# Last products of a two-layer encoder: token tile 0 through one unit sooner, its norm between tile 1's adds, part of tile 1's norm on TensorE, and another order of the first loads

## The chip, the core and the metric

The kernel runs on one core of a Trainium2 chip. The metric is device microseconds (us) of one execution, median of several runs; lower is better. All times are in us unless ns is written.

The engines: PE is TensorE's matrix product, PEld its weight load, DVE is VectorE, ACT is ScalarE, POOL is GpSimd, SP is SyncE, which issues most of the transfers (DMAs).

## The reference, cut to what matters

Two post-norm residual layers over 16 learned tokens and 256 frames of width 2048. Layer 0 mixes gated linear attention and stick-breaking attention, layer 1 is a state-space mixer. Each layer projects the tokens in, mixes, projects out, adds the result to the scaled input and normalizes:

```python
for layer in range(DEPTH):
    f = _even_mixer(h, ...) if layer % 2 == 0 else _odd_mixer(h, ...)
    h = _layer_norm(DEEPNORM_ALPHA * h + f, ln_g[layer], ln_b[layer])
return h[:, PREFIX:]

def _layer_norm(x, g, b):
    mu = jnp.mean(x, -1, keepdims=True)
    xc = x - mu
    var = jnp.mean(xc * xc, -1, keepdims=True)
    return xc * lax.rsqrt(var + LN_EPS) * g + b

def _odd_mixer(...):          # its end: 8 groups of 512 values each
    y = _rms_norm_groups(y * jax.nn.silu(z), norm_w, SSM_GROUPS)
    return jnp.einsum('bte,ed->btd', y, w_out)
```

The change touches two places: the very first projections of layer 0, and the last output products of layer 1 with the last layer norm.

## The kernel before

All matrix products are made from two parts of each float32 operand: a high part, which ACT copies into the format fp32r (`split_into`, line 146), and the low rest, which DVE or POOL subtracts (line 147). Three products, high-high, high-low and low-high, stand for one. The weights are cut into units of 128 x 2048 float32 (1 MB); a unit is loaded into one of three `raw` buffers, split in two halves of 1024 columns, and used by PE. The split of unit i+1 is emitted beside the products of unit i (`units`, line 390 on), and unit i+2 is loaded.

A planner that simulates the program orders the instructions of each engine; the order in the code is only a priority, unless it is pinned.

**The start** (`layer0`, line 258). ACT's queue issues the first 256 columns of units 0 to 2. SP's queue issues x rows 0 and 1 (one row is 128 of the 2048 input values for all tokens), then columns 256 to 512 of the three units, then rows 2 and 3 ("x1" in line 274), rows 4 and 5 ("x2"), the second quarter of each unit, and so on. The loop over c splits what has come and makes the products of two rows with three units. Before it, constants are set up: small tiles that POOL fills and, at line 311, 16 copies on DVE.

**The end** (`tail`, line 1209). Layer 1's output projection has 8 groups of 4 units; a unit gives 512 columns of the output, for two tiles of 128 tokens. `out1_half` (line 466) makes the products of half a unit for one tile, `out1_add` (line 480) adds the PSUM result, scaled per token, to the accumulator `acc`. For all groups but the last a unit serves both tiles before the next unit comes. In the last four units (i0 to i0+3, group g = 7) tile 0 goes through all four first, then tile 1. Each add is followed by `bn_stats`; after the fourth add the mean and variance are gathered (`bn_aggr`), the reciprocal deviation r comes from Ln and Exp on ACT and one Newton step of three DVE operations (line 253 on), and the 2048 columns are normalized in up to three pieces: columns c1 by two `scalar_tensor_tensor` on DVE (center: subtract the mean, times lg; scale: times r, plus lb), columns c0 by ACT (times r, minus mean times r) and then POOL (times lg, plus lb), columns c2 by ACT and then DVE. For tile 0, c0 and c1 have 1024 columns each; for tile 1, c0 has 320, c1 832 and c2 896. Each piece is stored by a DMA from SP's queue. Tile 1's last unit is made in two halves of 256 columns (`b`).

Products rotate through four PSUM buffers (`pj`); two more (`po`) serve smaller products.

## Time and profile before

| what | us |
| --- | --- |
| median of 3 runs (lowest to highest) | 1405.85 (1404.2 to 1406.54) |
| the profiled execution | 1404.02 |
| its span in the trace | 1402.3 |
| PE busy in the span | 1382.8 (99%) |
| DVE busy | 1024.5 (73%) |
| ACT busy | 769.0 (55%) |
| POOL busy | 324.2 (23%) |

Times within the trace count from the span's start. A row of a group gives an engine, an operation, its output and inputs, a count, the busy time and the mean of one; behind the bar stands how long the engine was idle before it and for whom it waited. PE's products are pipelined, so the end of one overlaps the start of the next.

### The profile page before, as it was taken

How to read it: one execution, taken by the hardware profiler on the slowest of the kernel's cores; microseconds unless marked ns; L12 is line 12 of the kernel's file. 1: busy time of each engine (PE TensorE's matmuls, PEld its weight loads, DVE VectorE, ACT ScalarE, POOL GpSimd, SP SyncE). 2: the span in 40 equal slices, each digit the busy share in tenths (PEclk: the TensorE clock that was granted, in tenths of full speed). 3: DMA queues.
4: the chain of work that ended last, by engine and by line, in shares of the span. 5: the costliest groups of instructions: out<-in, count | busy, mean ns of one | idle time of the engine just before them, and what ended most of it. 6: DMA issues, size and time to landing. Idle time of an engine off the chain costs nothing.

```text
span 1402.3 us, 26080 instructions
## 1 busy us (share of the span) xinstructions
PE 1382.8 (99%) x10701; PEld 1329.7 (95%) x10701; DVE 1024.5 (73%) x1663; ACT 769.0 (55%) x1138; POOL 324.2 (23%) x285
## 2 busy tenths in 40 slices
PE   9999999999999999999999999999999999999996
PEld 8999999999999999999999899899898999989985
DVE  7857575575565675558799989777887768778687
ACT  6645454364345544545587766555555565565651
POOL 0000110100101100114402325342332433424323
PEclk9999999999999999999999999999999999999998
DMA  9544444445444445444444755655556456454651
GB/s 326 183 153 165 168 155 176 165 167 172 159 172 160 151 154 192 156 155 142 151 151 172 265 175 192 213 192 178 207 175 227 154 192 218 161 204 149 222 196 61
DMA packets 37720, 249.84 MB, mean 178 GB/s; under 512 B 4256, under 2 KB 6112, under 8 KB 9184
## 3 DMA queue, kind: packets, MB, share of 16 engines
q1 hardware_dynamic: 37168, 247.77, 50.7%
q8 instruction: 84, 1.38, 0.4%
q10 hardware_dynamic: 432, 0.39, 0.1%
q14 instruction: 36, 0.29, 0.1%
HBM read 245.94 MB, written 2.20 MB: 177 GB/s over the span
## 4 chain that ended last, share of the span: by engine, by line
PE 83%; DVE 7%; ACT 4%; issue 2%; POOL 2%; DMA 1%; ACTq 0%; SPq 0%; POOLq 0%; DVEq 0%
PE pj L166 21%; PE pj L165 21%; PE pj L167 21%; PE pj L476 4%; PE pj L477 4%; PE pj L478 4%; DVE wlo L147 2%; PE po L1172 2%; ACT whi L146 1%; PE po L590 1%; DVE xlo L816 1%; POOL wlo L147 1%; DMA ebc<-edr 1%; DMA hacc<-in_xT 1%; POOL xt L1010 1%
## 5 line engine op out<-in xcount | busy, mean ns | idle before, releaser
L165 PE MATMUL pj<-xhi,whi 128*128 128x272 f32 (+4 forms) x2560 | 734.2, 287 | 1.5 <-ACT xhi L317 0.5
L166 PE MATMUL pj<-xlo,whi 128*128 128x272 f32 (+4 forms) x2560 | 731.3, 286 | 0.0
L167 PE MATMUL pj<-xhi,wlo 128*128 128x272 f32 (+4 forms) x2560 | 729.8, 285 | 0.0
L147 DVE TENSOR_TENSOR wlo<-raw,whi 128x1024 fp32r<-128x1024 f32 (+2 forms) x405 | 514.2, 1273 | 244.8 <-ACT whi L146 243.2
L146 ACT ACTIVATE whi<-raw 128x1024 fp32r<-128x1024 f32 (+2 forms) x435 | 451.1, 1038 | 396.4 <-PE pj L166 329.7
L165 PEld LDWEIGHTS pj<-xhi,whi 128*128 128x128 f32 x2560 | 481.6, 188 | 4.9 <-ACT whi L146 1.7
L166 PEld LDWEIGHTS pj<-xlo,whi 128*128 128x128 f32 x2560 | 482.6, 189 | 1.5 <-issue 0.6
L167 PEld LDWEIGHTS pj<-xhi,wlo 128*128 128x128 f32 x2560 | 482.0, 188 | 0.5 <-issue 0.4
L165 PE MATMUL pj<-mixh,whi 128*128 128x272 f32 x384 | 111.2, 291 | 1.0 <-ACT mixh L801 1.0
L167 PE MATMUL pj<-mixh,wlo 128*128 128x272 f32 x384 | 110.7, 289 | 0.0
L166 PE MATMUL pj<-mixl,whi 128*128 128x272 f32 x384 | 110.7, 289 | 0.0
L147 POOL TENSOR_TENSOR wlo<-raw,whi 128x1024 fp32r<-128x1024 f32 x30 | 75.7, 2524 | 118.7 <-ACT whi L146 118.5
L476 PE MATMUL pj<-whi,yh 128*128 128x512 f32 (+1 forms) x244 | 94.8, 388 | 0.0
L478 PE MATMUL pj<-whi,yl 128*128 128x512 f32 (+1 forms) x244 | 94.2, 386 | 0.0
L477 PE MATMUL pj<-wlo,yh 128*128 128x512 f32 (+1 forms) x244 | 94.2, 386 | 0.0
L248 POOL TENSOR_TENSOR gr<-gr,gsc 128x1088 f32<-128x1088 f32 x6 | 15.4, 2570 | 302.6 <-ACT gsc L247 302.6
L165 PEld LDWEIGHTS pj<-mixh,whi 128*128 128x128 f32 x384 | 72.2, 189 | 1.3 <-ACT mixh L801 1.1
L166 PEld LDWEIGHTS pj<-mixl,whi 128*128 128x128 f32 x384 | 72.3, 188 | 0.2
L167 PEld LDWEIGHTS pj<-mixh,wlo 128*128 128x128 f32 x384 | 72.3, 188 | 0.1
L485 DVE SCALAR_TENSOR_TENSOR acc<-pj,rr,acc 128x512 f32<-128x512 f32 (+1 forms) x65 | 46.1, 734 | 15.2 <-PE pj L478 15.1
L478 PEld LDWEIGHTS pj<-whi,yl 128*128 128x128 f32 x244 | 45.8, 188 | 9.2
L476 PEld LDWEIGHTS pj<-whi,yh 128*128 128x128 f32 x244 | 45.8, 188 | 9.1
(327 smaller groups left out, 1518.7 us busy)
## 6 DMA issues: line engine op xcount, KB each, us to landing
raw<-in_wts SPq DMA_DIRECT2D x212, 1024.0 KB, 4.8
ebc<-edr SPq DMA_DIRECT2D x8, 1664.0 KB, 6.4
raw<-in_wts SPq DMA_DIRECT2D x9, 256.0 KB, 5.7
hacc<-in_xT SPq DMA_DIRECT2D x7, 272.0 KB, 5.4
early<-in_wts SPq DMA_DIRECT2D x2, 512.0 KB, 7.1
lg<-in_lnr SPq DMA_DIRECT2D x1, 1024.0 KB, 4.5
lb<-in_lnr SPq DMA_DIRECT2D x1, 1024.0 KB, 4.5
out_h<-acc SPq DMA_DIRECT2D x2, 512.0 KB, 2.6
```

The costliest lines, as they stand in the source:

```text
L146: self.nc.scalar.activation(hi, src, AF.Copy)
L147: eng.tensor_tensor(lo, src, hi.bitcast(F32), op=ALU.subtract)
L165: mm(ps, whi, xhi, start=first, stop=False)
L166: mm(ps, whi, xlo, start=False, stop=False)
L167: mm(ps, wlo, xhi, start=False, stop=last)
L248: mul(c, c, e, op=ALU.mult)
L476: mm(ps, yh[:, kk, tt], hi[:, k, :], start=kk == 0, stop=False)
L477: mm(ps, yh[:, kk, tt], lo[:, k, :], start=False, stop=False)
L478: mm(ps, yl[:, kk, tt], hi[:, k, :], start=False, stop=kk == 3)
L485: self.nc.vector.scalar_tensor_tensor(a, ps, r[:, t : t + 1], a, op0=ALU.mult, op1=ALU.add)
L590: mm = lambda r, a, b, start=False, stop=False: self.nc.tensor.matmul(o[:, r], a, b, start=start, stop=stop, skip_group_check=True)
L1172: mm(o[i * 64 : (i + 1) * 64, jj, t0:S], xd[:, s, h * 64 : (h + 1) * 64], M[:, h, c0:c1], start=(s, jj) == (0, 0), stop=False, **gk,)
```

## The change

**Last products.** The unit before the last four (i0-1, the last of group 6) joins the tail: tile 0 goes through five units in a row, then tile 1. Five units are split ahead; the second half of unit i0 is put into two tiles of the old `xts` buffers and is subtracted on DVE, not POOL.

**Tile 0's norm** is a generator (`first_tile`) that is stepped after each of tile 1's adds: behind the last add of tile 0 the statistics, centering of columns 768 to 1408, Newton's step, ACT on columns 0 to 768 and POOL's two operations on them; behind the add of unit i0-1, centering of 1408 to 2048 and scaling of 768 to 1408; behind that of i0, tile 1's columns 0 to 512 times lg (`times_lg`) and the scaling of tile 0's 1408 to 2048; behind that of i0+1, tile 1's columns 512 to 768 times lg.

**Tile 1's norm.** Columns 0 to 768, already multiplied by lg, are finished on PE: the identity times acc, plus diag(-mean) times lg, plus diag(sd) times lb, in PSUM; ACT multiplies by r when it copies them out, and issues their DMAs from its own queue. DVE centers and scales the other 1280 columns.

**Order.** `keep_order` chains all DVE and all ACT instructions from tile 0's last unit on in the order of the code.

**First loads.** Rows 2 and 3 of x are issued before columns 256 to 512 of the weights, in one DMA as before; the constants are set up behind the split of the third round (`issue_after`).

The diff, with the body of the moved setup cut:

```diff
--- before.py
+++ after.py
@@ -121,6 +121,19 @@
         while self.side:
             self.tick()
 
+    def traced(self):
+        return self.tc.nc.cur_bb.bb.instructions
+
+    def keep_order(self, first):
+
+        ins = self.traced()
+        n0 = next(n for n in reversed(range(len(ins))) if ins[n] is first)
+        free = mybir.DependencyInfo(mybir.DependencyClass.NoSync, mybir.DependencyReason.DATA)
+        for eng in (mybir.EngineType.DVE, mybir.EngineType.Activation):
+            mine = [i for i in ins[n0:] if i.engine == eng]
+            for a, b in zip(mine, mine[1:]):
+                self.tc.add_manual_dep(b, a.name, free, reason="keep_order")
+
 
     def load_unit(self, i, q=None):
         if i >= NU:
@@ -269,9 +282,10 @@
             nc.scalar.dma_start(self.raw[u][:, :256], self.wts[u][:, :256])
         for kt in range(2):
             nc.sync.dma_start(self.hacc[:, kt, :], self.xT[:, kt, :])
+        nc.sync.dma_start(self.hacc[:, 2:4, :], self.xT[:, 2:4, :])
         for u in range(NS):
             nc.sync.dma_start(self.raw[u][:, 256:512], self.wts[u][:, 256:512])
-        for kind, n in ("x1", "x2", "w1", "x3", "x4", "w2", "x5", "x6", "w3", "x7"):
+        for kind, n in ("x2", "w1", "x3", "x4", "w2", "x5", "x6", "w3", "x7"):
             if kind == "x":
                 r = slice(2 * int(n), 2 * int(n) + 2)
                 nc.sync.dma_start(self.hacc[:, r, :], self.xT[:, r, :])
@@ -285,30 +299,6 @@
         self.load_wg2(0)
         nc.sync.dma_start(self.cpk[:, :C_END], self.cpk_d)
         nc.sync.dma_start(self.dta, self.dta_d)
-
-        self.nones_r, self.nL_r = [lp.tile([P, P], F32R, tag=n, name=n) for n in ("nones", "nL")]
...
-        for q in range(4):
-            for r in range(4):
-                vec.tensor_copy(add4[32 * q : 32 * q + 32, 32 * r : 32 * r + 32], self.ident[32 * q : 32 * q + 32, 32 * q : 32 * q + 32])
         self.guT = lp.tile([P, T], F32, tag="gsq", name="guT")
         self.guS = lp.tile([96, T], F32R, tag="guS", name="guS")
         ps = [self.pj() for _ in range(NS + 1)]
@@ -337,9 +327,36 @@
                 if c % 2 == 0:
                     for u in range(NS):
                         w_parts(u, c * 256, c * 256 + 512)
+            if c == 2:
+                mark = next(i for i in reversed(self.traced()) if i.engine == mybir.EngineType.DVE)
             for u in range(NS):
                 for kt in (2 * c, 2 * c + 1):
                     self.first_kt(ps[u][:, :T], u, kt)
+        with self.tc.issue_after(mark):
+
+            self.nones_r, self.nL_r = [lp.tile([P, P], F32R, tag=n, name=n) for n in ("nones", "nL")]
...
+            for q in range(4):
+                for r in range(4):
+                    vec.tensor_copy(add4[32 * q : 32 * q + 32, 32 * r : 32 * r + 32], self.ident[32 * q : 32 * q + 32, 32 * q : 32 * q + 32])
 
         for kt in range(KT):
             o = ps[NS][32 * (kt % 4) : 32 * (kt % 4) + 32, :T]
@@ -881,7 +898,7 @@
         nc.vector.memset(self.xd2, 0.0)
         self.rstd1 = {}
         self.first1()
-        self.units(len(L0), L1[:-4], {n: None for n in range(NFIRST)})
+        self.units(len(L0), L1[:-5], {n: None for n in range(NFIRST)})
         self.tail()
 
     def first1(self):
@@ -1210,16 +1227,21 @@
 
         nc, lp = self.nc, self.lp
         vec, pool = nc.vector, nc.gpsimd
+        act, mm = nc.scalar.activation, nc.tensor.matmul
         i0, g = NU - 4, NG - 1
         self.drain()
+        self.load_unit(i0 + 1)
+        self.split_half(i0, 0)
+        hi, lo = [lp.tile([P, 1024], F32R, tag="xts", name=self.nm("late"), bufs=2) for _ in range(2)]
+        self.split_into(self.raw[i0][:, 1024:], hi, lo, vec)
+        self.parts[i0, 1] = (hi, lo)
         self.load_unit(i0 + 2)
         for n, dq in enumerate((1, 2)):
             for h in range(2):
                 src = self.raw[i0 + dq][:, h * 1024 : (h + 1) * 1024]
                 o = slice((2 * n + h) * 1024, (2 * n + h + 1) * 1024)
                 hi, lo = [a.rearrange("p k t -> p (k t)")[:, o] for a in self.xrows]
-                nc.scalar.activation(hi, src, AF.Copy)
-                vec.tensor_tensor(lo, src, hi.bitcast(F32), op=ALU.subtract)
+                self.split_into(src, hi, lo, vec)
                 self.parts[i0 + dq, h] = (hi, lo)
             if n == 0:
                 self.load_unit(i0 + 3)
@@ -1229,43 +1251,107 @@
         nc.sync.dma_start(lb, self.lnr_d[1].partition_broadcast(P))
         for h in range(2):
             self.split_half(i0 + 3, h)
+
+        nid, dm = [lp.tile([P, P], F32, tag="ys2", name=self.nm("diag"), bufs=2) for _ in range(2)]
+        dsd = lp.tile([P, P], F32, tag="yu", name="dsd", bufs=2)
+        act(nid, self.ident, AF.Copy, scale=-1.0)
+        out = [self.out[t * P : (t + 1) * P, :] for t in range(2)]
+        accs = [self.acc[:, t, :] for t in range(2)]
+        sts = [lp.tile([P, 8, 6], F32, tag="fst", name=self.nm("fst"), bufs=2) for _ in range(2)]
+        mvs = [lp.tile([P, 2], F32, tag="fmv", name=self.nm("fmv"), bufs=2) for _ in range(2)]
+        sc = [[lp.tile([P, 1], F32, tag=f"f{n}", name=self.nm("f"), bufs=2) for n in range(4)] for _ in range(2)]
+
+        def center(t, a, b):
+            c = slice(a, b)
+            vec.scalar_tensor_tensor(
+                accs[t][:, c], accs[t][:, c], mvs[t][:, 0:1], lg[:, c], op0=ALU.subtract, op1=ALU.mult
+            )
+
+        def scale(t, a, b):
+            c = slice(a, b)
+            vec.scalar_tensor_tensor(accs[t][:, c], accs[t][:, c], sc[t][1], lb[:, c], op0=ALU.mult, op1=ALU.add)
+            nc.sync.dma_start(out[t][:, c], accs[t][:, c])
+
+        def times_lg(a, b):
+            vec.tensor_tensor(accs[1][:, a:b], accs[1][:, a:b], lg[:, a:b], op=ALU.mult)
+
+        def moments(t):
+            v, r, _, _ = sc[t]
+            vec.bn_aggr(mvs[t], sts[t])
+            vec.tensor_scalar(v, mvs[t][:, 1:2], LN_EPS, None, op0=ALU.add)
+            act(r, v, AF.Ln)
+            act(r, r, AF.Exp, scale=-0.5)
+
+        def first_tile():
+
+            N0, N1 = 768, 1408
+            v, r, tm, mr = sc[0]
+            moments(0)
+            center(0, N0, N1)
+            self.newton(r, v, tm)
+            vec.scalar_tensor_tensor(mr, mvs[0][:, 0:1], -1.0, r, op0=ALU.mult, op1=ALU.mult)
+            a = accs[0][:, :N0]
+            act(a, a, AF.Identity, bias=mr, scale=r)
+            pool.tensor_tensor(a, a, lg[:, :N0], op=ALU.mult)
+            pool.tensor_tensor(a, a, lb[:, :N0], op=ALU.add)
+            nc.sync.dma_start(out[0][:, :N0], a)
+            yield
+            center(0, N1, D)
+            scale(0, N0, N1)
+            yield
+            times_lg(0, 512)
+            scale(0, N1, D)
+            yield
+            times_lg(512, NP)
+            yield
+
+
+        NP = 768
+        side = None
         for t in range(2):
-            st = lp.tile([P, 8, 6], F32, tag="fst", name=self.nm("fst"), bufs=2)
-            acc = self.acc[:, t, :]
-            for dq in range(4):
-                halves = (0, 1) if t == 1 and dq == 3 else (None,)
-                for b in halves:
+            for dq in range(-1, 4):
+                u, gg = (i0 + dq, g) if dq >= 0 else (i0 - 1, g - 1)
+                col = dq % 4
+                if (t, dq) == (0, 3):
+                    first = self.traced()[-1]
+                for b in (0, 1) if (t, dq) == (1, 3) else (None,):
                     ps = self.pj()
                     for h in range(2):
-                        self.out1_half(ps, g, t, *self.parts[i0 + dq, h], h, b)
-                    self.out1_add(ps, g, t, dq, b)
-                    with self.tc.high_priority():
+                        self.out1_half(ps, gg, t, *self.parts[u, h], h, b)
+                    self.out1_add(ps, gg, t, col, b)
+                    if dq >= 0:
                         for c in range(2) if b is None else (b,):
-                            vec.bn_stats(st[:, 2 * dq + c, :], acc[:, dq * 512 + c * 256 : dq * 512 + (c + 1) * 256])
-            mv = lp.tile([P, 2], F32, tag="fmv", name=self.nm("fmv"), bufs=2)
-            v, r, tm, mr = [lp.tile([P, 1], F32, tag=f"f{n}", name=self.nm("f"), bufs=2) for n in range(4)]
-            with self.tc.high_priority():
-                vec.bn_aggr(mv, st)
-                vec.tensor_scalar(v, mv[:, 1:2], LN_EPS, None, op0=ALU.add)
-                nc.scalar.activation(r, v, AF.Ln)
-                nc.scalar.activation(r, r, AF.Exp, scale=-0.5)
-                self.newton(r, v, tm)
-                vec.scalar_tensor_tensor(mr, mv[:, 0:1], -1.0, r, op0=ALU.mult, op1=ALU.mult)
-            cut = (0, 1024, 2048, 2048) if t == 0 else (0, 320, 1152, 2048)
-            c0, c1, c2 = [slice(a, b) for a, b in zip(cut, cut[1:])]
-            vec.scalar_tensor_tensor(acc[:, c1], acc[:, c1], mv[:, 0:1], lg[:, c1], op0=ALU.subtract, op1=ALU.mult)
-            for c, eng in ((c0, pool), (c2, vec)):
-                if c.stop > c.start:
-                    a = acc[:, c]
-                    nc.scalar.activation(a, a, AF.Identity, bias=mr, scale=r)
-            vec.scalar_tensor_tensor(acc[:, c1], acc[:, c1], r, lb[:, c1], op0=ALU.mult, op1=ALU.add)
-            nc.sync.dma_start(self.out[t * P : (t + 1) * P, c1], acc[:, c1])
-            for c, eng in ((c0, pool), (c2, vec)):
-                if c.stop > c.start:
-                    a = acc[:, c]
-                    eng.tensor_tensor(a, a, lg[:, c], op=ALU.mult)
-                    eng.tensor_tensor(a, a, lb[:, c], op=ALU.add)
-                    nc.sync.dma_start(self.out[t * P : (t + 1) * P, c], a)
+                            vec.bn_stats(sts[t][:, 2 * dq + c, :], accs[t][:, dq * 512 + c * 256 : dq * 512 + (c + 1) * 256])
+                if t == 1 and side is not None:
+                    next(side, None)
+                if (t, dq) == (0, 3):
+                    side = first_tile()
+                    next(side)
+
+        acc, mv = accs[1], mvs[1]
+        v, r, tm, sd = sc[1]
+        qs = [slice(512, NP), slice(0, 512)]
+        pss = [self.po()[:, : q.stop - q.start] for q in qs]
+        pin = self.tc.keep_in_program_order
+        for ps, q in zip(pss, qs):
+            pin(mm(ps, self.ident, acc[:, q], start=True, stop=False))
+        moments(1)
+        act(dm, nid, AF.Copy, scale=mv[:, 0:1])
+        center(1, NP, 1216)
+        self.newton(r, v, tm)
+        vec.tensor_tensor(sd, v, r, op=ALU.mult)
+        act(dsd, self.ident, AF.Copy, scale=sd)
+        for d, a, l in ((dm, lg, False), (dsd, lb, True)):
+            for ps, q in zip(pss, qs):
+                pin(mm(ps, d, a[:, q], start=False, stop=l))
+        center(1, 1216, 1664)
+        center(1, 1664, D)
+        scale(1, NP, 1408)
+        scale(1, 1408, D)
+        for ps, q in zip(pss, qs):
+            act(acc[:, q], ps, AF.Copy, scale=r)
+            nc.scalar.dma_start(out[1][:, q], acc[:, q])
+        self.keep_order(first)
 
 
 def _pack(i):
```

## Rows read from the trace of the kernel before

**Rows 1.** The page: busy time, share of the span, instructions.
```profile
PE 1382.8 (99%) x10701; PEld 1329.7 (95%) x10701; DVE 1024.5 (73%) x1663; ACT 769.0 (55%) x1138; POOL 324.2 (23%) x285
```

**Rows 2.** Chain of waits, 1389 to 1403: start, us, engine, tile, line.
```profile
1390.92 0.49 DVE acc L485
...
1396.97 1.63 DVE acc L1267
```

**Rows 3.** DMA issues, 1330 to 1403: count, KB each, us to landing.
```profile
out_h<-acc SPq DMA_DIRECT2D x1, 448.0 KB, 2.7
```

**Rows 4.** Timeline of DVE and ACT at the end: start, us, operation [idle before].
```profile
1377.17 0.75 DVE L485 SCALAR_TENSOR_TENSOR acc<-pj,rr,acc 128x512 f32<-128x512 f32 x1 [1.19 <-PE pj L478]
...
1379.89 0.75 DVE L485 SCALAR_TENSOR_TENSOR acc<-pj,rr,acc 128x512 f32<-128x512 f32 x1 [1.18 <-PE pj L478]
1380.67 0.75 DVE L1244 BATCH_NORM_STATS2 fst<-acc 128x6 f32<-128x256 f32 x2
...
1381.94 1.27 DVE L1256 SCALAR_TENSOR_TENSOR acc<-acc,fmv,lg 128x1024 f32<-128x1024 f32 x1
...
1392.37 1.07 DVE L1256 SCALAR_TENSOR_TENSOR acc<-acc,fmv,lg 128x832 f32<-128x832 f32 x1
...
1392.72 0.20 ACT L1251 ACTIVATE f<-f 128x1 f32<-128x1 f32 x1
...
1393.74 0.16 DVE L255 SCALAR_TENSOR_TENSOR f<-f,f 128x1 f32<-128x1 f32 x1
```

**Rows 5.** Groups by shape, DVE and ACT: count, busy us, mean ns, idle before.
```profile
L253 DVE TENSOR_TENSOR f<-f 128x1 f32<-128x1 f32 x2 | 0.3, 150 | 0.0
L1266 DVE TENSOR_TENSOR acc<-acc,lg 128x896 f32<-128x896 f32 x1 | 1.1, 1092 | 0.8 <-ACT acc L1260 0.8
...
L943 ACT ACTIVATE acc<-po 128x512 f32<-128x512 f32 x8 | 4.7, 586 | 0.0
L544 ACT ACTIVATE ke<-ge 128x128 f32<-128x128 f32 x8 | 2.4, 302 | 0.0
L1260 ACT ACTIVATE acc<-acc,f,f 128x1024 f32<-128x1024 f32 x1 | 1.2, 1247 | 2.7 <-DVE f L1253 2.7
```

**Rows 6.** Chain of waits, 0 to 40: one float32 product, in two passes.
```profile
31.17 0.46 PE po L351 x2
```

**Rows 7.** Timelines of POOL and DVE: operations that overlap on both engines.
```profile
1361.98 2.83 POOL L147 TENSOR_TENSOR wlo<-raw,whi 128x1024 fp32r<-128x1024 f32 x1 [7.94 <-ACT whi L146]
1362.46 2.37 DVE L253 TENSOR_TENSOR rt<-rr 128x2 f32<-128x2 f32 x1
...
1368.44 3.53 POOL L147 TENSOR_TENSOR wlo<-raw,whi 128x1024 fp32r<-128x1024 f32 x1 [3.63 <-ACT whi L146]
...
1386.47 3.07 POOL L1266 TENSOR_TENSOR acc<-acc,lg 128x1024 f32<-128x1024 f32 x1 [14.50 <-ACT acc L1260]
1388.05 0.75 DVE L485 SCALAR_TENSOR_TENSOR acc<-pj,rr,acc 128x512 f32<-128x512 f32 x1
1389.62 2.38 POOL L1267 TENSOR_TENSOR acc<-acc,lb 128x1024 f32<-128x1024 f32 x1
```

**Rows 8.** Windows: busy us by engine, PE's granted clock, DMA share, GB/s.
```profile
1393.00:1393.50 0.50, 0.00 (x0) 0.00 (x0) 0.50 (x2) 0.00 (x0) 0.00 (x0) 0.96 1.07 442
1393.50:1394.00 0.50, 0.00 (x0) 0.00 (x0) 0.40 (x4) 0.00 (x0) 0.00 (x0) 0.50 0.99 410
```

**Rows 9.** The start: chain of waits, windows (PE, PEld, DVE, ACT, POOL), DVE's copies.
```profile
4.50 5.42 DMA hacc<-in_xT
...
11.92 0.39 PE pj L165
...
5.00:8.00 3.00, 2.47 (x15) 1.83 (x14) 2.94 (x14) 2.22 (x7) 0.00 (x0) 1.00 1.00 311
16.00:24.00 8.00, 8.00 (x64) 7.42 (x62) 5.47 (x8) 5.47 (x8) 0.00 (x0) 1.00 1.05 407
...
3.07 1.76 DVE L311 COPY add<-ident 32x32 f32<-32x32 f32 x16
```

More of the change, by code (lines that the diff above doesn't have):

```diff
@@ L342, in layer0 @@
                     self.first_kt(ps[u][:, :T], u, kt)
+        with self.tc.issue_after(mark):
+            self.nones_r, self.nL_r = [lp.tile([P, P], F32R, tag=n, name=n) for n in ("nones", "nL")]
+            nones, nL = [lp.tile([P, T], F32, tag="gs2", name=n, bufs=2)[:, :P] for n in ("nones_f", "nL_f")]
+            nc.gpsimd.memset(nones, -1.0)
+            nc.gpsimd.affine_select(
+                out=nL, in_=nones, compare_op=ALU.is_ge, fill=0.0, base=0, pattern=[[-1, P]], channel_multiplier=1
+            )
+            self.spad = lp.tile([P, 432], F32, tag="spad", name="spad")
+            v2 = [lp.tile([80, 512], F32R, tag=f"v2{i}", name=f"v2{i}") for i in range(2)]
+            s2 = [lp.tile([80, 1, 16], F32R, tag=f"s2{i}", name=f"s2{i}") for i in range(2)]
+            self.v2, self.s2 = v2, s2
+            self.sp2, self.nL2 = [lp.tile([48, n, 16], F32R, tag=t, name=t) for n, t in ((2, "sp2"), (1, "nL2"))]
+            add4 = lp.tile([P, 432], F32, tag="ge", name="add4")[:, :P]
+            selx = lp.tile([P, T], F32, tag="gk", name="selx_f")[:96, :P]
+            self.selx = lp.tile([P, T], F32R, tag="grs", name="selx")[:96, :P]
+            nc.gpsimd.memset(selx, 0.0)
+            for q in range(0, 96, 64):
+                nc.gpsimd.memset(selx[q : q + 1, :], 1.0)
+            for q in range(4):
+                for r in range(4):
+                    vec.tensor_copy(add4[32 * q : 32 * q + 32, 32 * r : 32 * r + 32], self.ident[32 * q : 32 * q + 32, 32 * q : 32 * q + 32])
         for kt in range(KT):
@@ new lines, in tail @@
+        out = [self.out[t * P : (t + 1) * P, :] for t in range(2)]
[7 more added lines that the diff above has]
+                accs[t][:, c], accs[t][:, c], mvs[t][:, 0:1], lg[:, c], op0=ALU.subtract, op1=ALU.mult
+            )
```

16 lines of the change are left out of this document (removed).

## The prediction

> **What bounds the kernel now.** I read the page first: TensorE (PE) is busy in 99% of the span, with no other engine above 73% [rows 1]. So a step beside the matrix products is worth nothing while they run, and only the two ends of the program are open. The chain of waits at the end shows the second one: the last add of a product starts on VectorE (DVE) at 1390.92, and from there to the last VectorE operation, which ends at 1398.60, everything is VectorE or ScalarE (ACT) work on tile 1's norm [rows 2]. The span ends at 1402.3, 3.7 us after that operation; the 448 KB that it releases land in 2.7 us of them [rows 3]. So the tail is 11.38 us after the last add's start (A below). At the other end the chain runs through x rows 4 and 5, which land at 9.92, and then through splits until PE has work without pause at 11.92 [rows 9].
>
> The profiled execution took 1404.02, span 1402.3; the median of the runs is 1405.85, 1.83 above it. I take differences from the trace and put them on the median.
>
> **What the products lose or gain: nothing.** The same products run; tile 0 takes five of them in a row instead of four, then tile 1 five. One product of a tile takes 2.72 (adds at 1377.17 and 1379.89 [rows 4]), so tile 0's last add can start at 1379.89 - 2.72 = 1377.17, and its norm has 13.6 instead of 10.9 us of products beside it. The splits are wanted 2.72 earlier; I price that at nothing, since the last of them, POOL's half of unit i0+3, ends at 1371.97 [rows 7] and its first use moves to about 1375.8; if it came late, PE would stall by what is lacking.
>
> **The new end, if the last add is on time.** Counted from A. Before, the centering starts at A+1.45 (1392.37) and the ScalarE Exp runs from A+1.80 to 2.00 [rows 4]. DVE durations: 1.27 for 1024 columns and 1.07 for 832 [rows 4], so 1.05 ns a column: 0.87 for 640, 0.67 for 448, 0.60 for 384; an independent successor starts 0.08 before the end. Then: center 448 to A+2.12; Newton's three operations A+2.05 to 2.58 (before, the third starts 1.37 after the centering, which has 832 columns there [rows 4]); sd 2.62 to 2.77; center 448 and 384 to 3.89; scale 640 to 4.68 and 640 to 5.47. Last DMA of this path: A+5.5.
> The other path: dm on ACT (0.30, as the 128x128 row [rows 5]) to A+2.33; PE's two products with it. The nearest row is a float32 product of 272 columns in 0.46 [rows 6], so 768 columns take 1.30: A+2.36 to 3.66. dsd needs sd, is ready at 3.10 and so hidden; its round runs 3.66 to 4.96. ACT empties 512 columns of PSUM in 0.59 [rows 5], and its DMA starts at A+5.6. The first round (identity times acc) follows PE's last product while DVE makes statistics, so costs nothing.
> Both paths end at about A+5.6, the old one at A+7.7 (1398.62). With the same 3.6 to the end of the span (1040 KB leave in four pieces; the last 256 KB go by the 448 KB row) the tail is 9.2 instead of 11.38: **2.2 us less**.
>
> **What the new order does to the last add.** ScalarE and VectorE keep program order from tile 0's last unit on, so each add of tile 1 is queued behind pieces of tile 0's norm. One thing takes no place in a plain sum. At 1361.98 GpSimd (POOL) starts a subtraction of two SBUF tensors; VectorE's 2-column multiply at 1362.46 then takes 2.37 instead of 0.15 [rows 5, 7] and ends with it, 1364.83 to 1364.81. PSUM adds are not held: the one at 1388.05 takes its usual 0.75 inside a POOL operation that runs to 1389.54 [rows 7]. The Trainium skill states this rule on its page "SBUF — State Buffer", section "SBUF: two separate sides": VectorE with two SBUF inputs and GpSimd exclude each other for a whole instruction. The trace agrees (2.37 against 0.15), and the rule speaks against this change, for scale and times_lg both have two SBUF inputs.
>
> With that, in the trace's clock: tile 0's last add 1377.17; centering 2.05 later, as from 1379.89 to 1381.94 [rows 4], at 1379.22; Newton 1380.01 to 1380.74; ScalarE's 768 columns (1.25 for 1024 [rows 5], so 1.0) to 1381.8, when POOL's multiply is ready. DVE: add of unit i0-1 at 1380.66 (its product was there at 1379.89), center 640 to 1382.19. POOL goes next and needs 0.75 of 2.38 [rows 7] = 1.8, to 1384.0; scale 640 waits for it and ends at 1384.87; POOL's addition then runs to 1386.67. Beside it DVE does add and statistics of the next unit (1384.79 to 1386.24, 0.75 and 0.75 [rows 4]), but times_lg of 512 columns waits from there to 1386.67 and ends at 1387.39 (0.72, from 1.09 for 896 [rows 5]); scale 640 ends at 1388.18. Then DVE alone: add and statistics 1388.10, times_lg of 256 (0.45) 1389.55, add and statistics 1389.92, the first half's 1391.37, the last add **1392.2**. Its product is there at 1390.92 as before: **1.3 us late**. Without the 2.2 us of holding the same sum has DVE waiting for the product by 1388.05, so no lateness. The bounds are 0 and 2.2; I take 1.3, for the 2.37 us row is the same pair of engines and kinds. PE does not stall for it: four PSUM buffers rotate, and the one wanted at 1389.4 is free from 1385.5.
>
> **The start.** x rows 2 and 3 are issued before the weights' second quarter, not behind it; all that is queued ahead of rows 4 and 5 is the same bytes. What can gain is 144 KB more in flight early (272 for 128): at 311 GB/s [rows 9], 0.46. What can lose: the third unit's quarter now has the place in SP's queue where x stood, behind a wait for the first loads; if ScalarE waits for it with x queued behind, the second round of products starts by one quarter's copy later, about 0.3 (128 columns take 0.30 [rows 5]). Rows 4 and 5 land long after, so this is mostly hidden; PE idles 0.53 of 5 to 8 as it is [rows 9]. I take -0.2, range -0.5 to +0.3. The moved setup (16 copies on DVE, 1.76 [rows 9], and the casts of the tiles that POOL fills) meets a later stretch where DVE is busy 5.47 of 8.00 and PE all of it [rows 9]; it costs nothing unless a copy stands before a split that PE wants, 1.76 for all of them.
>
> **Sum.** -2.2 + 1.3 - 0.2 = -1.1: profiled 1402.9, median 1405.85 - 1.1 = **1404.75**, say 1404.8.
>
> **Rivals.**
> 1. DVE and POOL miss each other (the POOL operations fall beside adds and statistics), and the last add is on time: -2.2 - 0.2 = -2.4, so 1403.4; with the start's best, 1403.1. Against it: the 2.37 row; for it: adds and statistics are some 60% of DVE's time in the sums above.
> 2. PE's clock falls before the corrections: slower. In the trace the last product ends at 1390.9, the granted clock is 0.96 in 1393.0 to 1393.5 and 0.50, the 1.2 GHz level, in the next half [rows 8]. With A at 1392.2 the first correction starts at 1394.5, later than that fall. Only the identity round, done at 1392.2, stands between. If it does not hold the clock, both rounds take 2.6 each: last DMA at A+8.2, tail 11.8, so +0.4 + 1.3 - 0.2 = +1.5: 1407.3. It decides from the point where the clock falls before about 1394.5; if it falls between the rounds, the result is near 1406.
> 3. The planner, given other sizes and an order it may not change, lets PE wait at the start or for a split in the last units: up to 2.7, so 1406 to 1409. For it: DVE cannot step round a late operation any more; against: the last split has 3.8 us to spare.
> 4. The new order of loads has no effect at all because the same bytes come first: 1405.0, inside the forecast's range.
>
> **How the numbers follow.** Forecast with rival 4: 0.52. Rival 1: 0.24. Rival 2: 0.14. Rival 3: 0.10. 0.2% is 2.8 us, about what a measurement of this kernel can tell from no change: faster means under 1403.0, slower over 1408.7. Rival 1 passes the first bound in somewhat under half of its weight, the forecast in a sixth: 0.20. Rival 3 passes the second in a third, rival 2 in a seventh: 0.06. The rest, 0.74, is no change. The range 1402.4 to 1407.6 takes in both bounds of the lateness, the start's range and rival 2's price.
>
> **What the changed profile would show.** Scale of tile 0 on DVE as a record of 2 us or more that ends after POOL's multiply; the last add more than 1 us after PE's last product; a tail of 9.2 from that add; granted clock of 1.0 while the six correction passes run; PE without pause before 12 us as late as now. I would be wrong first at the lateness: if the last add follows its product at once, the gain doubles.

## The result: 0.14% slower, not the little faster that was forecast

| | before | changed |
|---|---|---|
| median of the runs, us | 1405.30 (22 runs, 1403.99 to 1407.30) | 1407.03 (22 runs, 1405.13 to 1409.43) |
| ratio, 95% interval | | 1.0014, 1.0008 to 1.0020 |
| profiled execution, us | 1404.02 | 1406.69 |
| its span, us | 1402.3 | 1405.0 |

The forecast was 1404.8, 1.1 us less than the 1405.85 of the first three runs of the kernel before; measured are 1.7 us more than the 1405.30 of all 22. The profiled executions differ by 2.7. Four marks in each trace say where that went: G, the start of VectorE's (DVE's) copy of the gate products, which waits for the last of the first products; F, the start of the first add of an output product of layer 1; A, the start of the last add; E, the end of the span.

| stretch | before | changed | difference |
|---|---|---|---|
| start to G | 28.07 | 29.06 | +0.99 |
| G to F (all of layer 0, first third of layer 1) | 875.04 | 877.10 | +2.06 |
| F to A (output products, norm of tile 0) | 487.81 | 489.06 | +1.25 |
| A to E (the tail) | 11.39 | 9.76 | -1.63 |

The new end does gain, 0.4 us net in these two executions. The start loses 1.0, and 2.1 are lost in a place that the diff does not touch. All rows of this section are from the trace of the changed kernel unless it is said otherwise. The page's first line answers to [rows 1]:

```profile
PE 1387.7 (99%) x10713; PEld 1332.7 (95%) x10713; DVE 1027.4 (73%) x1669; ACT 769.2 (55%) x1141; POOL 317.7 (23%) x282
```

**The start** answers to [rows 9]. The waits of TensorE (PE) between 0 and 30 us (engine, tile, line; releaser; us in total, times, longest):

```profile
PE pj L178 <- ACT whi L159: 1.1, 1, 1.1
...
PE pj L179 <- DVE xlo L308: 0.6, 1, 0.6
```

The windows there (stretch, then busy us of PE, weight loads, DVE, ScalarE (ACT), GpSimd (POOL), granted clock, DMA share, GB/s):

```profile
5.00:8.00 3.00, 3.00 (x23) 2.69 (x22) 2.57 (x8) 2.52 (x7) 0.00 (x0) 1.00 0.93 303
...
10.00:12.00 2.00, 0.77 (x5) 0.34 (x3) 0.94 (x2) 1.28 (x3) 0.00 (x0) 1.00 1.03 373
12.00:16.00 4.00, 3.35 (x25) 3.14 (x25) 3.87 (x21) 3.13 (x5) 0.00 (x0) 1.00 1.05 403
```

PE is busy in all of 5 to 8 us where it was in 2.47 of 3.00, and rows 2 and 3 of x do come sooner: ACT starts their split at 5.88, before at 7.79. But PE then runs out of work, 0.77 of 2.00 busy and 3.35 of 4.00. The first wait, 1.1 us, is for a high part of weights (`whi`) whose load lands no sooner than before (ACT splits it from 10.71, before from 10.60). What PE waits for last is the low part of a split of x (`xlo`), and DVE's timeline (start, us, operation, idle before) shows what stands in front of that split:

```profile
11.38 1.94 DVE L160 TENSOR_TENSOR wlo<-raw,whi 128x512 fp32r<-128x512 f32 x3 [1.06 <-ACT whi L159]
13.23 1.22 DVE L359 COPY add<-ident 32x32 f32<-32x32 f32 x11
14.48 0.72 DVE L308 TENSOR_TENSOR xlo<-hacc,xhi 128x544 fp32r<-128x544 f32 x1
```

Eleven of the sixteen 32x32 copies, 1.22 us in one piece, ran before the `xlo` of 14.48. Before, DVE had little room there, as its window shows:

```profile
12.00:16.00 4.00, 4.00 (x33) 4.00 (x34) 3.92 (x7) 3.80 (x7) 0.00 (x0) 1.00 1.05 406
```

**The middle.** PE's waits between 735 and 836 us, the kernel before and then the changed one:

```profile
PE po L1172 <- DVE M L1074: 1.8, 1, 1.8
```

```profile
PE z L1078 <- POOL bc L1027: 2.2, 1, 2.2
PE po L1001 <- DVE dt_scr L993: 0.8, 1, 0.8
PE po L1189 <- DVE xd L1141: 0.6, 1, 0.6
PE po L1215 <- POOL ysq L1209: 0.5, 1, 0.5
```

1.8 us of waiting became 4.1. The code of this stretch, the first groups of layer 1, is the same in both kernels, but the planner laid the engines' queues out in another order there. POOL's timelines show the largest piece of it, before and then changed:

```profile
796.32 1.33 POOL L1010 TENSOR_TENSOR bc<-bc,xcl 128x528 f32<-128x528 f32 x1 [2.10 <-ACT xcl L1009]
797.60 1.73 POOL L1183 TENSOR_TENSOR yu<-yu,gz 128x256 f32<-128x256 f32 x1
```

```profile
795.04 3.92 POOL L1200 TENSOR_TENSOR yu<-yu,gz 128x256 f32<-128x256 f32 x2 [5.37 <-DVE yu L1199]
798.93 1.48 POOL L1027 TENSOR_TENSOR bc<-bc,xcl 128x528 f32<-128x528 f32 x1
```

Before, the product `bc` goes first, as soon as its input `xcl` is there, and two `yu` behind it. In the changed order two `yu` go first and hold POOL until 798.96; `bc` follows at 798.93, though ACT had finished its input at 795.91, and PE's `z` product is what waits 2.2 us for it:

```profile
795.28 0.63 ACT L1026 ACTIVATE xcl<-xcl 128x528 f32<-128x528 f32 x1
```

**The end** answers to [rows 2, 4, 7]. PE's last product ends at 1394.56. The pair that the prediction spoke of, and the last add, on DVE and POOL:

```profile
1384.93 0.88 DVE L1266 SCALAR_TENSOR_TENSOR acc<-acc,fmv,lg 128x640 f32<-128x640 f32 x1
1385.72 2.47 DVE L1272 SCALAR_TENSOR_TENSOR acc<-acc,f,lb 128x640 f32<-128x640 f32 x1
...
1389.68 0.77 DVE L1276 TENSOR_TENSOR acc<-acc,lg 128x512 f32<-128x512 f32 x1
...
1395.22 0.47 DVE L502 SCALAR_TENSOR_TENSOR acc<-pj,rr,acc 128x256 f32<-128x256 f32 x1
```

```profile
1385.49 2.02 POOL L1295 TENSOR_TENSOR acc<-acc,lg 128x768 f32<-128x768 f32 x1 [10.41 <-ACT acc L1294]
1387.59 2.30 POOL L1296 TENSOR_TENSOR acc<-acc,lb 128x768 f32<-128x768 f32 x1
```

The chain of waits behind the last add (start, us, what):

```profile
1395.73 0.44 DVE fst L1324
...
1396.19 0.38 DVE fmv L1280
...
1396.78 0.21 ACT f L1282
...
1397.02 0.20 ACT f L1283
1397.22 0.30 ACT diag L1339
...
1397.56 2.00 PE po L1346 x6
...
1399.59 0.48 ACT acc L1352
...
1400.49 0.69 ACT acc L1352
```

The windows while the corrections run answer to [rows 8]:

```profile
1397.00:1398.00 1.00, 0.44 (x2) 0.41 (x3) 0.90 (x6) 0.49 (x2) 0.00 (x0) 1.00 0.00 0
...
1399.50:1400.00 0.50, 0.50 (x3) 0.08 (x1) 0.50 (x2) 0.41 (x1) 0.00 (x0) 1.00 0.00 0
```

The granted clock is 1.00, the 2.4 GHz level, through all of them.

### The profile page after: what moved, and what is told of

Same layout as the page of the kernel before. It is cut to its first block, busy times and chain, and to the rows that moved or that the text cites. A ratio compares the mean times of both kernels' runs of the same rounds, so it can differ in the third digit from the quotient of the medians.

```text
span 1405.0 us, 26105 instructions
## 1 busy us (share of the span) xinstructions
PE 1387.7 (99%) x10713; PEld 1332.7 (95%) x10713; DVE 1027.4 (73%) x1669; ACT 769.2 (55%) x1141; POOL 317.7 (23%) x282
## 4 chain that ended last, share of the span: by engine, by line
PE 83%; DVE 8%; ACT 3%; issue 3%; POOL 2%; DMA 1%; SPq 0%; ACTq 0%; POOLq 0%; DVEq 0%
PE pj L179 22%; PE pj L178 21%; PE pj L180 21%; PE pj L493 4%; PE pj L494 4%; PE pj L495 4%; DVE wlo L160 2%; PE po L1189 1%; PE po L607 1%; ACT whi L159 1%; DVE xlo L833 1%; POOL wlo L160 1%; DVE xt L1016 1%; POOL xt L1027 1%; ACT hacc L946 1%
## 5 line engine op out<-in xcount | busy, mean ns | idle before, releaser
L160 POOL TENSOR_TENSOR wlo<-raw,whi 128x1024 fp32r<-128x1024 f32 x29 | 71.4, 2464 | 122.5 <-ACT whi L159 122.3
```

Of the source, the lines that this page charges most:

```text
L160: eng.tensor_tensor(lo, src, hi.bitcast(F32), op=ALU.subtract)
```

## The experiments

Each kernel ran 11 times beside the kernel before, the changed one 22 times. The medians of the kernel before beside them were 1405.18 (the four that take the change apart), 1405.27 (order held, late copies with it, the two other ends), 1405.45 (late copies with the order free, both repaired, mean's diagonal first) and 1405.76 (one line altered). The marks of the profiled executions, with the number of short stretches at the 1.2 GHz level between G and F, of which the last section tells:

| kernel | median | ratio (95%) | G | G to F | F to A | A to E | low clock |
|---|---|---|---|---|---|---|---|
| before | | | 28.07 | 875.04 | 487.81 | 11.39 | 0 |
| changed | 1407.03 | 1.0014 (1.0008 to 1.0020) | 29.06 | 877.10 | 489.06 | 9.76 | 0 |
| new end alone | 1405.42 | 0.9994 (0.9985 to 1.0003) | 27.68 | 877.65 | 489.04 | 9.91 | 2 |
| new start alone | 1408.27 | 1.0020 (1.0012 to 1.0029) | 28.54 | 879.59 | 488.26 | 11.50 | 3 |
| loads alone | 1407.68 | 1.0014 (1.0005 to 1.0022) | 28.61 | 877.47 | 488.27 | 11.51 | 1 |
| moved setup alone | 1405.99 | 1.0008 (0.9999 to 1.0017) | 29.02 | 875.53 | 487.83 | 11.61 | 0 |
| new start, order held | 1406.65 | 1.0009 (1.0000 to 1.0017) | 29.36 | 875.16 | 488.22 | 11.39 | 0 |
| the same, late copies | 1405.12 | 0.9995 (0.9987 to 1.0004) | 27.63 | 876.20 | 488.60 | 11.61 | 1 |
| late copies, order free | 1405.05 | 0.9995 (0.9986 to 1.0003) | 27.88 | 874.84 | 487.84 | 11.61 | 0 |
| new end, POOL's part cut | 1404.54 | 0.9993 (0.9984 to 1.0002) | 28.70 | 876.86 | 488.40 | 9.93 | 1 |
| new end, other tail | 1404.77 | 0.9996 (0.9987 to 1.0005) | 28.43 | 875.42 | 489.02 | 10.14 | 0 |
| whole change, both repaired | 1404.12 | 0.9990 (0.9981 to 0.9999) | 28.51 | 876.57 | 488.63 | 9.90 | 1 |
| the same, mean's diagonal first | 1404.84 | 0.9997 (0.9989 to 1.0006) | 27.68 | 876.98 | 489.07 | 9.87 | 1 |
| whole change, one line altered | 1403.26 | 0.9984 (0.9975 to 0.9993) | 28.47 | 875.33 | 489.06 | 9.90 | 0 |

### Which part of the change loses

**The new end alone**: the diff without its two hunks in `layer0`.

> The new end with the start of before. Theory: the start alone costs 3.5 us of the changed kernel (1.0 by 16 us, 2.5 more between 750 and 831 us), and the new end gains what its own rows say: 11.38 from last add to end becomes 9.8, less 0.7 that the last add comes late, so -0.9: about 1404.4, PE's last product near 1390.9 as before. Rival: the longer run of tile 0 or the pinned order of the end delays the products themselves; then the last product is late here too and the time is near 1407.

**The new start alone**: those two hunks and nothing else.

> The new start (order of the first loads and the moved 16 copies) with the end of before. Theory: products 1.0 late at 16 us and 3.5 late from 831 us on, end as before: +3.5, about 1408.8. Rival (the end is to blame): within 1 us of before.

**The loads alone**, and **the moved setup alone**:

```diff
+        nc.sync.dma_start(self.hacc[:, 2:4, :], self.xT[:, 2:4, :])
         for u in range(NS):
             nc.sync.dma_start(self.raw[u][:, 256:512], self.wts[u][:, 256:512])
-        for kind, n in ("x1", "x2", "w1", "x3", "x4", "w2", "x5", "x6", "w3", "x7"):
+        for kind, n in ("x2", "w1", "x3", "x4", "w2", "x5", "x6", "w3", "x7"):
```

> Only the order of the first loads; the 16 copies stay ahead of everything. Theory: the 1.0 at 16 us is the copies, so it is gone (0.0 to 0.2 late at 16 us); the planner still orders the stretch from 750 to 831 us anew, so some 2.4 are lost there: +2.5, about 1407.8. Rival: the stretch in the middle loses because the start is late; then nothing is lost there, and the time is that of before.

> Only the 16 copies moved behind the third round's split; loads as before. Theory: the copies stand in front of a split that PE waits for, 0.9 to 1.2 late at 16 us; the middle gets yet another order from the planner, whose price is not known (0 to 3). So +1 to +4. Rival: the loss at the start is the order of the loads, and nothing is lost at 16 us here.

The end alone is not slower: its ratio of 0.9994 has an interval that reaches over 1, though its median stands 0.24 above that of the kernel before. The gain of 0.9 that was expected of it is not shown by the time. The start alone is slower by 0.20%, more than the whole change. So the loss is the start's. Its halves don't lose alike. The moved setup has the late first products (G 29.02) and a middle like that of before (875.53). The loads alone have a G of 28.61, and lose in the middle. But their G to F has a short stretch at the lower clock in it as well, so its 877.47 can't be put down to the order alone, and the runs below have to tell what the middle costs.

### Is it the planner's order, or a stream that comes late?

Names and numbers of layer 1's instructions are the same in both kernels, so the order of DVE, ACT, PE and SP can be held to that of the kernel before, by dependencies between neighbours on a queue that put no semaphore in (POOL's queue is left free, and came out in the order of before too):

```diff
+        for row in ORDER:
+            mine = [ins[f"I-{n}"] for n in row]
+            for a, b in zip(mine, mine[1:]):
+                self.tc.add_manual_dep(b, a.name, free, reason="order_of_before")
```

> The new start with the old end, as in the run of the new start alone, but the order of VectorE, ScalarE, TensorE and SyncE from the first unit of layer 1 on is held to that of the kernel before, instruction by instruction, with dependencies that add no semaphore. Theory (the planner, given a start that it reckons otherwise, lays out 750 to 831 us in another order, and that order costs some 2 us): the first products stay 1.0 us late, as before, but the step between 750 and 831 us goes, and the time is 1406.0 to 1406.5 where the new start alone took 1408.3; the waits of a z product on POOL's bc (2.2 us) and of a y product on dt_scr go. Rival (a stream that comes 1 us late meets its transfers and its buffers worse, in whatever order): the step stays, and the time is 1407.8 to 1408.5.

The new start, order held: PE's waits between 735 and 836 us are those of the kernel before again, though its stream comes 1.3 us late (G 29.36):

```profile
PE po L1267 <- DVE M L1169: 1.9, 1, 1.9
```

G to F is 875.16, against 875.04 before and 877.10 in the changed kernel, with the same clock in all three. The median falls from 3.1 us over the kernel before to 1.4; some of that fall may be clock, whose mean over the runs is 0.9955 in the new start alone and 0.9964 here. The rival (a late stream meets its buffers worse in any order) would have kept the step; it falls. What is left, 1.4 by the medians and 1.3 by G, was expected as 1.0.

### Are the copies the late start?

```diff
-            if c == 2:
+            if c == 7:
                 mark = next(i for i in reversed(self.traced()) if i.engine == mybir.EngineType.DVE)
```

> As the run before it, with the held order in layer 1, but the sixteen small copies (and what else is set up with them) may stand on VectorE only behind the last split of x for the first products, not behind that of the third pair of tiles. Theory (11 copies, 1.2 us in one piece, stand before a split of x that TensorE waits for, and that is the 1.0 us of the start): the first products are no more than 0.5 us late against before, and the time is 1404.8 to 1405.8. Rival (the other order of the loads and the conversions that stayed early on VectorE set the start): still 1.0 us late behind 15 us, 1406.0 to 1406.5, as in the run with the held order.

With the copies behind the last split of x, G is 27.63 and the median 0.15 under the kernel before: the late start is gone, with the loads in their new order and POOL's early fills and their conversions where the changed kernel has them. The copies now stand behind the last `xlo`:

```profile
20.83 0.72 DVE L386 TENSOR_TENSOR xlo<-hacc,xhi 128x544 fp32r<-128x544 f32 x1 [1.45 <-ACT xhi L385]
21.47 1.76 DVE L437 COPY add<-ident 32x32 f32<-32x32 f32 x16
```

One G decides little, since it varies by 0.9 to 1.0 between executions of one start, but all of them agree. The four with the mark at the third round (changed, new start alone, moved setup alone, order held) have a mean of 29.00, and in each of them PE waits 0.6 to 0.7 us for an `xlo`; in none of the other ten does it wait for one. So the copies were it. The four executions that have the late copies and the new loads besides this one give G of 28.51, 27.68, 27.88 and 28.47; the five together have a mean of 28.03. The four with the old start (before, new end alone, and its two variants) have 28.07, 27.68, 28.70 and 28.43, mean 28.22. The loads' own gain would then be 0.2 us, less than G varies between executions of one and the same start (27.63 to 28.51), and the run of the loads alone, with 28.61, shows none. No gain of theirs is shown.

The same late copies, with the planner left free in layer 1:

> New start with the copies behind the last split of x, old end, and the planner left free in layer 1 (it lays out the stretch from the first products of layer 1 in a fourth order, neither that of before nor that of the new start or of the copies alone). Beside the run with the held order (1405.12), this is the price of the planner's order alone. Theory (the order there has a price of its own that hangs on what the planner reckons of the start, and not on how late TensorE really is): first products 0.4 us sooner as in the held run, then a step in 750 to 831 us of between 0.3 and 3 us, 1405.4 to 1408. Rival (the step comes of a late start): no step, 1405.1.

No step: G to F is 874.84, the shortest of all, and the median is that of the held order. The planner's order here is a fourth one, and in it PE waits 1.8 us in the stretch, as before. I had expected some price for any new order, between 0.3 and 3 us. So a new order is not dear as such; the one that the changed kernel got is, and that of the late copies is not.

### The end: does POOL hold DVE, and what is the tail made of?

```diff
-            pool.tensor_tensor(a, a, lg[:, :N0], op=ALU.mult)
-            pool.tensor_tensor(a, a, lb[:, :N0], op=ALU.add)
+            pool.tensor_tensor(a[:, :16], a[:, :16], lg[:, :16], op=ALU.mult)
+            pool.tensor_tensor(a[:, :16], a[:, :16], lb[:, :16], op=ALU.add)
```

> The new end with the old start, as in the run of the new end alone, but POOL's product and sum on tile 0's first 768 columns are cut to 16 columns (752 columns of tile 0 are so left without scale and offset). Theory (POOL holds VectorE while both work: the scale of 640 columns took 2.47 us beside POOL where one of that size alone takes some 0.85, and the last adds are late by what is left of it): the first scale takes about 0.85, the last add starts within 0.15 us of the end of its product instead of 0.66, and the time is 0.5 to 0.7 us under that of the new end alone. Rival (VectorE has simply too much to do between the last products, POOL or not): the last add stays 0.4 us or more late, and the time is that of the new end alone, 1405.4.

DVE's timeline of this kernel, the scale that took 2.47 and the last add:

```profile
1385.08 0.88 DVE L1268 SCALAR_TENSOR_TENSOR acc<-acc,f,lb 128x640 f32<-128x640 f32 x1
...
1391.09 0.75 DVE L498 SCALAR_TENSOR_TENSOR acc<-pj,rr,acc 128x512 f32<-128x512 f32 x1 [0.39 <-PE pj L491]
...
1393.96 0.48 DVE L498 SCALAR_TENSOR_TENSOR acc<-pj,rr,acc 128x256 f32<-128x256 f32 x1 [0.49 <-PE pj L491]
```

0.88 instead of 2.47, and now DVE waits for PE ahead of the last adds (0.39 and 0.49, in brackets) instead of coming 0.66 late. The mechanism is shown. `times_lg` of 512 columns takes 0.69 in this run. The time, 0.9 us under the new end alone by the medians, agrees with it, but the two ratios, 0.9993 and 0.9994, can't be told apart.

```diff
-        moments(1)
-        act(dm, nid, AF.Copy, scale=mv[:, 0:1])
+        vec.bn_aggr(mv, sts[1])
+        vec.tensor_scalar(v, mv[:, 1:2], LN_EPS, None, op0=ALU.add)
+        act(dm, nid, AF.Copy, scale=mv[:, 0:1])
+        act(r, v, AF.Ln)
+        act(r, r, AF.Exp, scale=-0.5)
...
+        vec.tensor_scalar(acc[:, 256:512], pss[1][:, 256:], r, None, op0=ALU.mult)
+        nc.sync.dma_start(out[1][:, 256:512], acc[:, 256:512])
```

> The new end with the old start, and two steps of the end in another order: the diagonal of the mean is made on ScalarE before the logarithm and the exponential (it needs the mean alone), and the last 512 columns of tile 1 are taken out of PSUM in two halves, by ScalarE and by VectorE, instead of by ScalarE in one piece. Theory (behind the last add stands a chain: statistics, diagonal, products, copy out, transfer): the first product by the diagonal starts 0.4 to 0.5 us sooner behind the last add (2.34 us in the run of the new end alone), the second diagonal comes 0.2 later, the last copy ends 0.2 to 0.3 sooner, and from the last add to the end it is 9.3 to 9.5 us instead of 9.93; 1404.9 to 1405.1. Rival (the transfers out set the end, or the second diagonal does): 9.8 to 10.1 us, 1405.4.

A miss: 10.14 instead of 9.3 to 9.5. The first correction did come 0.46 sooner behind the last add (1.88 for 2.34), but DVE's half of the copy stands behind its two scales, at A + 5.57, and its transfer is the third in SyncE's queue. The work moved to the longer path.

### Both costs repaired

> The whole change, with its two suspected costs taken out: the small copies may stand on VectorE only behind the last split of x for the first products, and layer 1's order on the four engines is held to that of the kernel before. Theory (the change lost by these two alone, and its start and its end each bring something): the first products are 0.4 to 0.8 us sooner than before, no step between 750 and 831 us, the end as in the profile of the changed kernel (last add 0.6 late, tail 9.8), together 1 to 2 us under the kernel before where no stretch of low clock falls in: 1403.5 to 1404.8. Rival (start and end do not add up, since products that come sooner only meet other limits): 1405.0 to 1405.4, as before.

> As the run before it, and the diagonal of the mean is made on ScalarE ahead of the logarithm and the exponential, with the last 512 columns still copied out by ScalarE in one piece. In the run where VectorE took half of them out, the first product by the diagonal came 1.88 us behind the last add (2.34 before) but the last transfer was issued by SyncE behind two others, 6.1 us behind the last add. Theory: from the last add to the end 9.6 to 9.7 us instead of 9.8 to 9.9, the time 0.1 to 0.3 us under that of the run before it, 1403.3 to 1404.6, too little to be told apart by the time. Rival (the second diagonal sets the end): no change in the tail.

With the copies late and the order held, the whole change is just faster than the kernel before: 1404.12, ratio 0.9990 (0.9981 to 0.9999). Its 11 runs have the mean granted clock of the changed kernel's 22 (0.9983 and 0.9984), and the mean times are 1404.30 and 1407.21, so the 2.9 us between them can hardly be clock, and they agree with the 1.0 and 2.1 of the two costs. The first products did not come 0.4 to 0.8 sooner than before, as expected; G is 28.51 here and 28.07 before.

The same with the mean's diagonal first is a miss: its interval reaches over 1, and the tail moves from 9.90 to 9.87 only. The last copy starts 0.21 sooner behind the last add (5.06 for 5.27), but its transfer takes longer to land, 2.6 us in the run before it and 2.8 in this one:

```profile
out_h<-acc ACTq DMA_DIRECT2D x1, 256.0 KB, 2.6
```

```profile
out_h<-acc ACTq DMA_DIRECT2D x1, 256.0 KB, 2.8
```

Why it does is open; in both runs the DMA share is 1.04 from 1400 to 1401, with DVE's two pieces still on their way out. The expected 0.2 is not there.

> The whole change with one line of it altered: the small copies may stand on VectorE only behind the last split of x (the mark is taken in the eighth round of the loop instead of the third); nothing is held, and the planner lays layer 1 out as in the run of the late copies without a held order. Theory (start and order of layer 1 were the loss; in that order TensorE waits 1.8 us between 735 and 836 us, as before, and not 4.1): the new end's 1 us is left over, 1403.6 to 1404.8, like the run with both costs repaired. Rival (the held order was what brought that run under the kernel before): 1405.0 to 1406.

The last kernel is the changed one with `c == 7` for `c == 2` and nothing held. PE's waits in it, 735 to 840 us:

```profile
PE po L1215 <- POOL ysq L1209: 1.1, 1, 1.1
PE po L1189 <- DVE xd L1141: 0.7, 1, 0.7
```

1403.26, ratio 0.9984 (0.9975 to 0.9993): 2.5 us under the kernel before by the medians, 0.3 below what was expected. With one line of it altered, the change beats the kernel before. That it also beats the run with both costs repaired (mean time 1403.29 against 1404.30) need not come of the free order: the mean granted clock of its runs is 0.9994 against 0.9983, and 0.0011 of 1403 is 1.5 us, as an estimate.

## Why the prediction was wrong, point by point

**The place where the sum failed: what it priced at nothing.** Two steps.

*The moved setup.* The prediction put the copies at nothing "unless a copy stands before a split that PE wants, 1.76 for all of them". Eleven of the sixteen, 1.22 us, did. It named the condition and the price and then let neither into the sum or into the start's range of -0.5 to +0.3. The row that argued for it (DVE busy 5.47 of 8.00 between 16 and 24 us [rows 9]) is from the wrong stretch: the mark is the third round of splits, and the copies ran from 13.23, where DVE is busy 3.92 of 4.00 in the trace of before. Measured: +0.99 in G between the two profiled executions, 29.00 against 28.22 by the means, and 28.03 with the mark moved. PE had work without pause from 15.26, where the prediction looked for it before 12.

*The middle.* "A step beside the matrix products is worth nothing while they run" is true of a step, but the prediction made of it that nothing could change between the two ends. It had a rival in which the planner lets PE wait, with a chance of 0.10 and 1406 to 1409, where the median lies; but it looked for it "at the start or for a split in the last units". It came at 735 to 836 us, 2.3 us more of waits and 2.1 in the marks: 99% busy [rows 1] still leaves 1.8 us of waits there, and the order of the queues that decides them is made from the planner's own reckoning of everything ahead of it. The held order shows that the order and not the late stream is the cause. Which property of the planner's reckoning made the dear order is not settled; the runs show four orders, with 1.8 us of waits in the stretch (before), 1.9 (moved setup alone), 1.8 (late copies) and 4.1 (changed). In the runs of the start and of the loads alone, which have the changed kernel's order there, the waits are 2.1 and 2.6; PE had come there later by a stretch at the lower clock, and so had less to wait for. That last reading is argued, not tried.

**The new end: right in its mechanism, wrong in both sizes, and right in its net by luck.** The last add was forecast 1.3 late and came 0.66 late; the tail was to fall by 2.2, to 9.2, and fell by 1.6, to 9.8. Over all executions of the table, F to A has a mean of 488.12 with the old end (seven) and of 488.98 with the new one and POOL's whole part (six); A to E 11.52 and, without the run with the other tail, 9.87. Net -0.8, forecast -0.9: two errors of 0.6 cancelled. Where the terms were off:

- *The hold.* In kind it is as forecast: the scale took 2.47, where centering as many columns took 0.88, and ended 0.68 behind POOL's product, which it had started beside. The prediction had 1.8 of holding there and 0.4 more at `times_lg`, 2.2 in all, of which 0.9 went into waits that DVE has anyway. Measured are 1.6 and 0.1 (0.77, against 0.69 in the run with POOL's part cut), 1.7 in all. The 0.9 is the same (0.39 and 0.49 of waits with POOL's part cut), and 0.8 is left, near to the 0.66. By the Trainium skill's page "SBUF — State Buffer", section "SBUF: two separate sides", the two operations should start only when POOL's ends. That makes ends of 1388.39 for the scale and 1390.58 for `times_lg`, and the trace agrees nearly: they came 0.20 and 0.13 sooner.
- *The tail.* The diagonal of the mean was ready at A + 2.30, forecast 2.33. The two rounds took 2.85 instead of 2.60: scaling the 272-column row [rows 6] to 768 columns was 10% short. The copy of 512 columns took 0.69 instead of 0.59. So the last DMA is issued at A + 5.99 instead of A + 5.6, and from there to the end it is 3.8 instead of the 3.6 that was kept (the prediction's own times, 1398.62 and 1402.3, give 3.7): the last transfer has 256 KB where it had 448, and lands no sooner for it (2.6 and 2.7 us [rows 3]).

**Rival 2, the falling clock: fell.** The granted clock was 1.00 in every window from 1397 to 1400, with PE idle from 1395.86 to 1397.56. Before, it had fallen 2.5 us after the last product [rows 8]. That the identity round between held it, as the prediction had it as the condition, agrees with this but was not tried: no run left that round out.

**The loads: not shown.** -0.2 was forecast. The means of G give 0.2, within what G varies, and the loads alone have a later G than before, 28.61. Rows 2 and 3 came sooner, but the next weights did not, so PE waited there instead; rival 4, no effect, can't be told apart.

**The range and the chances.** 1402.4 to 1407.6 held the median, but by luck: its upper part was there for rivals 2 and 3, with other causes and places. The forecast's sign was wrong: two unpriced steps of +1.0 and +2.1 stood against a gain of about 1.

## What to carry to other kernels

Where a planner orders the queues, a change at one place can reorder a stretch hundreds of microseconds behind it: compare the waits of the bounding engine over the whole span, or hold the old order, before a loss is put down to the lines that were edited. Setup that is moved "behind" a point must be moved behind the last operation that the bounding engine waits for, not behind some operation of that series: one number in one line was the difference between 0.14% slower and 0.16% faster, though a higher mean clock has a share in that. And a price that was worked out with its condition belongs in the range, even where the condition looks unlikely.

## What the runs showed of the hardware that I had not expected

Between executions of the same queues the granted clock differs in the middle of the run. Around 688 us PE pauses two or three times for some tenths, in every execution. The windows there, the kernel before and then the new end alone, whose queues are the same as before up to the last products:

```profile
686.00:688.00 2.00, 1.66 (x12) 1.11 (x10) 1.10 (x3) 1.72 (x4) 0.00 (x0) 1.00 0.91 385
688.00:690.00 2.00, 1.46 (x7) 0.95 (x8) 1.64 (x2) 0.80 (x3) 0.00 (x0) 1.00 0.04 16
690.00:692.00 2.00, 2.00 (x16) 1.92 (x15) 0.73 (x1) 1.80 (x4) 0.00 (x0) 1.00 0.79 229
```

```profile
686.00:688.00 2.00, 0.81 (x3) 0.32 (x3) 0.99 (x3) 2.00 (x4) 0.00 (x0) 1.00 0.81 340
688.00:690.00 2.00, 1.82 (x8) 1.30 (x9) 1.38 (x2) 0.48 (x3) 0.00 (x0) 0.78 0.20 25
690.00:692.00 2.00, 2.00 (x8) 1.77 (x8) 0.95 (x1) 1.89 (x4) 0.00 (x0) 0.50 0.85 291
```

In the second one PE was busy 0.81 of 2.00 in 686 to 688, where it was 1.66 before, and the granted clock falls behind it: 0.78, then 0.50, the 1.2 GHz level, with 8 products in 690 to 692 where there were 16. Seven of the fourteen profiled executions have one to three such stretches, each starting within 1.5 us of the end of a pause of PE (around 689, 734, 774 or 803 us). Of the executions that have before's order in the middle, the three without one (before, order held, other tail) have a G to F of 875.04 to 875.42, and the five with one or two 876.20 to 877.65. That is as large as the effects under study, so a single execution's span was no measure here, and medians and marks had to stand together. Around 688 us it fell in six of the eleven executions in which PE pauses three times (0.6, 0.2 and 0.7 us), and in none of the three with the last two pauses alone. What decides in which of the eleven it falls is open; no run tried it. It is not chance between executions alone: over the eleven runs of each, the mean granted clock is 0.9994 in the change with one line altered and 0.9983 in the run with both costs repaired and in the new end alone, whose ends are the same, while the kernel before stayed at 0.9961 to 0.9964 beside them.
